# Attention layer of a two-layer trunk: from a hand-woven TensorE order to a list scheduler that orders every queue, and the output projection's depth cut 6 + 2 in place of 7 + 1

## The chip, the cores and the metric

One Trainium2 chip, of which the kernel uses one core. The time is device microseconds of one execution, from the median of several runs. Five engines work side by side, each through a queue of its own: TensorE (PE: matrix products and transposes, with its weight loads PEld), VectorE (DVE), ScalarE (ACT), GpSimd (POOL) and SyncE (SP), which here only starts DMA transfers. What orders them against each other are semaphores.

## The reference

Layer A is gated DeltaNet with a gated ConvFFN, layer B chunked attention with a second ConvFFN. The change lies in the attention of layer B. There `h` is 1024 positions of 1024 channels, 16 heads are 64 wide, and every 64-position chunk sees itself and the eight chunks before it:

```python
kv = rmsnorm(h, kv_norm) @ w_kv
def chunk_attention(xn, w_q, rel_bias, w_out, k_pad, v_pad):
    q = (xn @ w_q).reshape(bsz, nc, CHUNK, B_HEADS, B_HEAD_DIM).transpose(1, 0, 2, 3, 4)
    ...
    def one_chunk(args):
        n, q_n = args
        k_band = lax.dynamic_slice_in_dim(k_pad, n * CHUNK, BAND, axis=1)
        v_band = lax.dynamic_slice_in_dim(v_pad, n * CHUNK, BAND, axis=1)
        s = jnp.einsum("bqhd,bkhd->bhqk", q_n, k_band) * scale + bias
        s = jnp.where(valid, s, NEG_INF)
        p = jax.nn.softmax(s, axis=-1)
        return jnp.einsum("bhqk,bkhd->bqhd", p, v_band)
    ...
    return o @ w_out
h = h + chunk_attention(rmsnorm(h, b_norm[j]), b_w_q[j], b_rel_bias[j], b_w_out[j], k_pad, v_pad)
h = h + conv_ffn(rmsnorm(h, f_norm[layer]), f_w_up[layer], f_conv[layer], f_conv_b[layer], f_w_down[layer])
```

## The kernel before

**Products in three parts.** Every fp32 operand is split into a high part and a low part (the rest). A product is three matmuls, high by high, high by low, low by high: lines L120, L121 and L122 of `dense`, 128x128 weights against 512 columns. `split_w` makes a weight tile's parts: optionally a fold of the norm's gain into the raw weights (L100 on POOL), the high part by ACT (L103), the low part by POOL (L105).

**Attention.** The heads are taken as eight pairs `p`. `queue_kv(p)` queues three dense tiles for each pair, K, Q and V, each of 48 matmuls (two halves `s` of 512 positions, eight blocks of depth); ACT and DVE cut the sums into high and low parts (`post_k`, `post_q`, `post_v`), and V is transposed by PE (L1995). A pair has eight units (head `a` of two, `tp` of four; a unit is two query tiles of 128 positions). For each query tile `scores` makes the scores on PE (L2042, L2043, into the PSUM tile `sc`, of which there is one), the sum with the bias and the row maximum on DVE (L2046), the exponential on ACT (L2048), a reciprocal on DVE (L2049) and the product with it on POOL (L2050, the tile `sS`). `attend` then transposes the shares on PE (L2070, tile `ptp`, two banks), splits them by ACT (L2080, `pTh`) and DVE (L2081, `pTl`), and multiplies by V (L2099, L2100, tile `poT`, one bank). `finish` adds the two halves of `poT` through ACT (L2104, `tm`) and DVE (L2105, `oT`). The first product of a unit can begin only when the `oT` of the unit before has read the one `poT` bank.

**What sets the order.** On PE the order is the program's: the `Weave` puts dense matmuls between a unit's steps by fixed credits (`more`, 1 to 2.2 dense steps of three matmuls at each hook). A pair's three dense tiles may start only once the pair two before it has stored its output (`("o", p - 2)`). ACT, DVE, POOL and SP are ordered by the framework's list scheduler.

**Output projection.** The outputs of pairs 0 to 6 go to DRAM and come back (`early_o`, 12 + 2 loads into the three buffers of the tag `vt`), when pair 5 is done. ACT and DVE or POOL split them (`split_act`, L338, L339). The first part takes seven blocks of depth of eight (`first_parts`, `part`); `rest(s)` adds the eighth when the last pair's half `s` is there: eight sums of three matmuls, each added to `h` on DVE (L459), squared on ACT (L357) and summed on DVE (L359, L367) for the norm before the ConvFFN. Eight tiny matmuls (L370, `pss`) total these sums. Between `rest(0)` and `rest(1)` stand the second halves of four parts.

**The ConvFFN behind it** has an order of its own, all engines in program order. Its first weights `r` are loaded from the POOL queue (L1437, `j == 0`).

Of the kernel before, what the change touches and what calls it, by code (L numbers as in the profile page):

```python
# [16 lines left out]
P = 128  # L17
# [11 lines left out]
def trunk_kernel(  # L29
# [170 lines left out]
    class Flow(Weave):  # L200
# [4 lines left out]
        def __init__(self):  # L205
            super().__init__()
            self.T, self.free, self.aux = 0.0, dict(D=0.0, A=0.0, G=0.0), deque([[0.0], [0.0]])
            self.time, self.items, self.last, self.stalls = {}, [], 0, []
            self.auto, self.tick, self.slack, self.cur, self.nxt, self.units = True, 0, 0.5, None, deque(), 0
            self.brief, self.split_at = False, 8  # L210
# [61 lines left out]
        def _dense(self):  # L272
            if self.cur is None:
# [8 lines left out]
                self.cur, self.split_at, self.units = e[0], e[4], 0  # L282
            try:
                next(self.cur)
            except StopIteration:
                self.cur = None
# [1066 lines left out]
    def ffn(layer, h, hp, xs, tail, d_r, last):  # L1353
# [80 lines left out]
        def load(j, q, t_=None):  # L1434
            t_ = t_ or room(j, q)
            k0, m = 4 * (q % 10 - 1), j if q < 20 else FP + j
            (nc.gpsimd if j == 0 else nc.sync).dma_start(out=t_, in_=w_up[k0 * P : (k0 + 4) * P, m * P : (m + 1) * P].rearrange("(k p) m -> p k m", p=P))  # L1437
# [513 lines left out]
    with ExitStack() as ph:  # L1951
        odd = ctx_o.enter_context(tc.tile_pool(name="bp1", bufs=1, **SB))
        bp = ph.enter_context(tc.tile_pool(name="bp", bufs=1, **SB))
        early_bp = ExitStack()
# [11 lines left out]

        def queue_kv(p):
# [4 lines left out]
            def post_k(s, ps):  # L1972
# [3 lines left out]
                for a, (r, r2) in enumerate(own):  # L1976
                    nc.scalar.copy(kA[a][r, c], ps[r])
                    nc.vector.tensor_tensor(kA[a][r2, c], ps[r], kA[a][r, c].bitcast(F32), op=ALU.subtract)

            def post_q(s, ps):  # L1980
# [4 lines left out]
                for a, (r, r2) in enumerate(own):  # L1985
                    nc.scalar.activation(qA[a][r, c], ps[r], AF.Copy, scale=0.125)
                    nc.vector.scalar_tensor_tensor(qL[a][r, c], ps[r], 0.125, qA[a][r, c].bitcast(F32), op0=ALU.mult, op1=ALU.subtract)
                    nc.vector.tensor_copy(qA[a][r2, c], qA[a][r, c].bitcast(F32))
                if s == 1:
                    wv.mark(("kq", p))  # L1990

            def turn(s, vt):
                pv = pB.tile([P, 4, P], F32, name="pvt", tag="pt", bufs=2)
                for t in range(4):
                    nc.tensor.transpose(pv[:, t], vt[:, t * P : (t + 1) * P], ident)  # L1995
                for a in range(2):
                    vs = kv["v"][a][:, 4 * s : 4 * s + 4, :]
                    src = pv[:, :, 64 * a : 64 * a + 64]
                    nc.scalar.copy(vs[:, :, 0:64], src)
                    nc.vector.tensor_tensor(vs[:, :, 64:128], src, vs[:, :, 0:64].bitcast(F32), op=ALU.subtract)  # L2000
                if s == 1:
                    wv.mark(p)
                yield

            def post_v(s, ps):
# [4 lines left out]
                t0 = wv.now  # L2010
                wv.short.append((lambda: True, lambda: t0 + 3, turn(s, vt)))
# [6 lines left out]
            for src, c0, g, post in ((w_kv, p * P, g_kv, post_k), (b_w_q, p * P, g_b, post_q), (w_kv, 1024 + p * P, g_kv, post_v))[2 if p == 0 else 0 :]:  # L2018
                load = lambda src=src, c0=c0, g=g: load_w(src, c0, fold=g, on_act=p < 1)
                wv.dense.append((lambda: p < 2 or ("o", p - 2) in wv.at, lambda: 0, dense_gen(load, post)))  # L2020
# [10 lines left out]
        def scores(a, t, kA, qA, qL, bt):  # L2031
# [7 lines left out]
            qs = slice(t * P, (t + 1) * P)  # L2039
            for i in range(n):  # L2040
                c = slice(k0 + i * w, k0 + (i + 1) * w)
                mm(ps[:, i, 0:w], qA[a][:, qs], kA[a][:, c], start=True, stop=False)  # L2042
                mm(ps[:, i, 0:w], qL[a][:, qs], kA[a][:, c], start=False, stop=True)  # L2043
            S = bp.tile([P, n, w], F32, name="sS", tag="sS", bufs=6)
# [3 lines left out]
            nc.scalar.activation(S, S, AF.Exp, bias=st[:, 1:2], accum_out=st[:, 2:3])  # L2048
            nc.vector.reciprocal(st[:, 3:4], st[:, 2:3])  # L2049
            nc.gpsimd.tensor_scalar(S, S, st[:, 3:4], 1.0, op0=ALU.mult, op1=ALU.mult)  # L2050
            return S.rearrange("p n w -> p (n w)"), t - nk + 1

        def attend(a, tp, kv, sc, oT, more, tail):

            kt0, kt1 = sc[0][1], 2 * tp + 1
            blocks = [((kt, 0), (kt, 1)) for kt in range(sc[1][1], 2 * tp + 1)]
            if sc[1][1] > kt0:
                blocks.append(((kt0, 0), (kt1, 1)))
            else:
                blocks.append((None, (kt1, 1)))  # L2060
            V = kv["v"]
            po = [None]

            def turn(bl):
                pt = pB.tile([P, 2, 256], F32, name="ptp", tag="pt", bufs=2)
                for j, b in enumerate(bl):
                    for e in b:
                        if e is not None:
                            S, s0 = sc[e[1]]
                            nc.tensor.transpose(pt[:, j, e[1] * P : (e[1] + 1) * P], S[:, (e[0] - s0) * P : (e[0] - s0 + 1) * P], ident)  # L2070
                pTh = bp.tile([P, 2, 256], F32R, name="pTh", tag="pTh", bufs=3)
                pTl = bp.tile([P, 2, 256], F32R, name="pTl", tag="pTl", bufs=3)
                if bl[-1][0] is None:
                    v = [(0, slice(0, 256)), (1, slice(P, 256))] if len(bl) == 2 else [(0, slice(P, 256))]
                    v = [(pt[:, j, c], pTh[:, j, c], pTl[:, j, c]) for j, c in v]
                else:
                    n = len(bl)
                    v = [(pt[:, 0:n], pTh[:, 0:n], pTl[:, 0:n])]
                for s_, h_, l_ in v:
                    nc.scalar.copy(h_, s_)  # L2080
# [239 lines left out]
```

## Time and profile before

| what | us |
|---|---|
| median of 3 runs (2609.0 to 2610.76) | 2609.09 |
| span of the profiled execution | 2612.5 |
| attention, 1371 to 1790 us of the span | 419 |
| change to the output projection, 1790 to 1830 us | 40 |
| projection's end and step to the ConvFFN, 1890 to 1930 us | 40 |
| start of the ConvFFN, 1930 to 2050 us | 120 |

The span is that of one execution under the profiler, from the first to the last instruction; it is 3.4 us above the median of the runs without it. In the views a row names the source line, the engine, the operation, and `out<-in` by the program's tile names. PE's matmuls are pipelined: in a list in order of time, the difference of two starts is what a matmul costs, while the duration beside it includes the pipeline.

### The profile page before, as it was taken

The page shows a single profiled execution, that of the slowest core. Times are in us where ns is not written, and L with a number is a line of the kernel's source. Part 1 is how long each engine was busy: PE and PEld are TensorE (multiplying, and loading weights), DVE is VectorE, ACT ScalarE, POOL GpSimd, SP SyncE. Part 2 cuts the span into 40 slices and gives each one's busy share as a digit, 9 for nine tenths or more (in the row PEclk, how much of TensorE's full clock was granted, in tenths as well). Part 3 has the DMA queues.
Part 4 walks back from the last instruction along what each step waited for, and adds up shares of the span by engine and source line. Part 5 has one row for each costly group of instructions (what it writes and reads, how often), then busy time and mean ns, then how long its engine had stood idle before and what let it go on. Part 6 is the DMA issues. An engine that isn't in the chain of part 4 may idle for free.

```text
span 2612.5 us, 39401 instructions
## 1 busy us (share of the span) xinstructions
PE 2520.3 (96%) x13933; PEld 2075.8 (79%) x13933; DVE 1857.8 (71%) x3102; ACT 1414.5 (54%) x2714; POOL 1486.5 (57%) x1472
## 2 busy tenths in 40 slices
PE   7999999999999999999999999999989999999998
PEld 5878888888777888887778888887867788888877
DVE  5755775454688888888775666666478788888875
ACT  5444555474455565555455555555345655555643
POOL 3655554346347777777645444443343777777771
PEclk9999999999999999999999999999999999999999
DMA  4534445455237777767831111114232567677785
GB/s 128 140 96 120 119 121 164 135 183 160 83 89 153 145 156 153 146 143 158 197 112 51 44 59 43 48 42 145 70 122 68 142 137 150 145 155 156 157 193 174
DMA packets 317590, 326.72 MB, mean 125 GB/s; under 512 B 32976, under 2 KB 240592, under 8 KB 317392
## 3 DMA queue, kind: packets, MB, share of 16 engines
q1 hardware_dynamic: 285936, 219.07, 28.2%
q0 software_dynamic: 26560, 96.48, 20.8%
q10 hardware_dynamic: 4896, 8.65, 0.9%
q8 instruction: 110, 1.80, 0.3%
q14 instruction: 88, 0.72, 0.1%
HBM read 180.94 MB, written 143.20 MB: 124 GB/s over the span
## 4 chain that ended last, share of the span: by engine, by line
PE 52%; DVE 5%; POOL 5%; issue 3%; DMA 2%; ACT 2%; SPq 0%; DVEq 0%; POOLq 0%; ACTq 0%
PE pu L1393 8%; PE pu L1392 8%; PE pu L1391 8%; PE pd L1393 4%; PE pd L1392 4%; PE pd L1391 4%; PE acc L120 3%; PE acc L121 3%; PE acc L122 3%; POOL ul L1358 2%; PE ptp L2070 2%; DMA r<-in_f_w_up_dram 1%; PE poT L2100 1%; PE poT L2099 1%; PE sc L2042 1%
## 5 line engine op out<-in xcount | busy, mean ns | idle before, releaser
L1358 POOL TENSOR_TENSOR ul<-r,uh 128x512 fp32r<-128x512 f32 x282 | 445.1, 1598 | 297.3 <-ACT uh L1379 282.4
L120 PE MATMUL acc<-xh,whi 128*128 128x512 f32 x896 | 375.6, 420 | 0.3 <-ACT xh L1097 0.2
L105 POOL TENSOR_TENSOR wlo<-wraw,whi 128x256 fp32r<-128x256 f32 (+1 forms) x293 | 236.8, 837 | 214.1 <-ACT whi L103 182.8
L122 PE MATMUL acc<-xh,wlo 128*128 128x512 f32 x896 | 353.4, 394 | 3.7 <-POOL wlo L105 3.7
L121 PE MATMUL acc<-xl,whi 128*128 128x512 f32 x896 | 354.1, 395 | 1.9 <-POOL xl L379 1.0
L1379 ACT CAST uh<-r 128x512 fp32r<-128x512 f32 x296 | 181.8, 622 | 222.1 <-DVE r L1358 154.0
L1393 PE MATMUL pu<-xh,ul 128*128 128x512 f32 x552 | 216.5, 392 | 6.2 <-POOL ul L1358 6.1
L1391 PE MATMUL pu<-xh,uh 128*128 128x512 f32 x552 | 216.3, 392 | 3.0 <-ACT uh L1379 1.5
L1392 PE MATMUL pu<-xl,uh 128*128 128x512 f32 x552 | 215.9, 391 | 1.0 <-POOL xl L379 1.0
L122 PEld LDWEIGHTS acc<-xh,wlo 128*128 128x128 f32 x896 | 169.1, 189 | 42.0 <-POOL wlo L105 4.5
L1712 ACT COPY stage<-pd 128x1024 f32<-128x1024 f32 x180 | 175.0, 1013 | 49.4 <-PE pd L1393 49.4
L121 PEld LDWEIGHTS acc<-xl,whi 128*128 128x128 f32 x896 | 170.4, 190 | 27.1 <-DVE xl L1098 3.1
L120 PEld LDWEIGHTS acc<-xh,whi 128*128 128x128 f32 x896 | 170.1, 190 | 23.3 <-ACT xh L1097 1.2
L1486 DVE SCALAR_TENSOR_TENSOR val<-vpre,colt,val 128x1023 f32<-128x1023 f32 (+2 forms) x92 | 153.2, 1665 | 38.6 <-ACT val L1483 38.4
L1358 POOL TENSOR_TENSOR dl<-a,dh 128x512 fp32r<-128x512 f32 x90 | 155.0, 1722 | 38.5 <-ACT dh L1379 38.5
L1486 DVE SCALAR_TENSOR_TENSOR gate<-gpre,colt,gate 128x1023 f32<-128x1023 f32 (+2 forms) x92 | 175.4, 1907 | 0.8
L2050 POOL TENSOR_SCALAR sS<-sS,st 128x640 f32<-128x640 f32 (+4 forms) x128 | 87.8, 689 | 143.1 <-DVE st L2049 122.9
L1358 DVE TENSOR_TENSOR r<-r,r 128x512 f32<-128x512 f32 x168 | 131.8, 784 | 31.1 <-POOL ul L1358 29.7
L2048 ACT ACTIVATE sS<-sS,st 128x640 f32<-128x640 f32 (+4 forms) x128 | 89.2, 696 | 82.0 <-DVE st L2047 80.2
L1393 PEld LDWEIGHTS pu<-xh,ul 128*128 128x128 f32 x552 | 104.0, 188 | 31.7 <-POOL ul L1358 10.4
L1391 PEld LDWEIGHTS pu<-xh,uh 128*128 128x128 f32 x552 | 103.9, 188 | 25.7 <-ACT uh L1379 2.4
L1392 PEld LDWEIGHTS pu<-xl,uh 128*128 128x128 f32 x552 | 104.0, 188 | 23.6 <-POOL xl L379 2.1
(389 smaller groups left out, 7110.0 us busy)
## 6 DMA issues: line engine op xcount, KB each, us to landing
r<-in_f_w_up_dram SPq DMA_DIRECT2D x168, 256.0 KB, 4.2
d_r<-stage POOLq DMA_DIRECT2D x78, 512.0 KB, 7.8
d_c<-stage POOLq DMA_DIRECT2D x70, 512.0 KB, 8.2
a<-in_f_w_down_dram SPq DMA_DIRECT2D x72, 256.0 KB, 2.7
wraw<-in_a_w_in_dram SPq DMA_DIRECT2D x32, 512.0 KB, 4.6
d_e<-stage POOLq DMA_DIRECT2D x32, 512.0 KB, 8.6
wraw<-in_a_w_out_dram SPq DMA_DIRECT2D x16, 512.0 KB, 4.2
d_r<-h ACTq DMA_DIRECT2D x32, 256.0 KB, 4.0
```

The lines of the kernel that those rows point to most:

```text
L105: nc.gpsimd.tensor_tensor(lo[:, c], raw[:, c], hi[:, c].bitcast(F32), op=ALU.subtract)
L120: mm(ps, hi[:, kw, wcol : wcol + P], rh[k][s], start=st, stop=False)
L121: mm(ps, hi[:, kw, wcol : wcol + P], rl[k][s], start=False, stop=False)
L122: mm(ps, lo[:, kw, wcol : wcol + P], rh[k][s], start=False, stop=sp)
L1358: tt = lambda eng, o, a, b, op: eng.tensor_tensor(o, a, b, op=op)
L1379: copy(hi, src)
L1391: mm(ps, w[0][:, cw], x[0], start=first, stop=False, skip_group_check=True)
L1392: mm(ps, w[0][:, cw], x[1], start=False, stop=False, skip_group_check=True)
L1393: mm(ps, w[1][:, cw], x[0], start=False, stop=last, skip_group_check=True)
L1486: nc.vector.scalar_tensor_tensor(t_[:, a:c1], p_[:, a - step : c1 - step], w[:, 2 - step : 3 - step], t_[:, a:c1], op0=ALU.mult, op1=ALU.add)
L1712: nc.scalar.copy(t_, ps)
L2048: nc.scalar.activation(S, S, AF.Exp, bias=st[:, 1:2], accum_out=st[:, 2:3])
```

## The change

The attention and the output projection are now written as generators for `Flow`, the list scheduler that the kernel uses for its first layer. `Flow` keeps a clock `T` of PE work and a time at which DVE, ACT and POOL come free (`on(e, cost)`), and takes, at each point, the highest-ranked item whose inputs it holds to be there, else one dense step. `score_run`, `turn_run` and `apply_run` are three such runs over all 64 units: up to six score tiles and three turned pieces may be open. Low parts are issued when the high part is due (`later`). The order in which items are taken is the program's order on all five queues (`manual_schedule()` without a list of engines).

Beside that:

- K and Q of a pair wait for the scores of the pair two before it (`("scored", p - 2)`), only V for its output. Each weight tile is loaded one tile ahead and split halfway through the tile before it.
- The first V tile's fold moves from ACT to POOL; the low parts of the projection's weights are cut in four pieces.
- The outputs of pairs 0 to 5 are fetched as each is stored, into six buffers of their own (`yo`); pair 6 is split straight from its tile, like pair 7.
- The projection's first part has six blocks of depth (`NO = 6`), `rest(s)` two: eight sums of six matmuls, with weights in two pieces.
- `h` comes back in eight loads of 512 KB in place of sixteen of 256 KB.
- In the second layer the ConvFFN's first four weight loads are started from SP in place of POOL.

The core of the diff:

```diff
-            (nc.gpsimd if j == 0 else nc.sync).dma_start(out=t_, in_=w_up[...])
+            (nc.gpsimd if j + layer == 0 else nc.sync).dma_start(out=t_, in_=w_up[...])
...
+        def kv_tile(src, c0, g, post):
+            raw = wp.tile(shape, F32, name="wraw", tag="wraw", bufs=2)
+            nc.sync.dma_start(out=raw, in_=src[:, c0 : c0 + P].rearrange("(k p) m -> p k m", p=P))
+            yield
+            wt = split_w(raw, shape, fold=g)
+            wv.on("G", 2.75, wv.on("A", 1.0, wv.on("G", 2.6)))
+            yield
+            for s in range(2):
+                ps = pacc.tile([P, HALF], F32, name="acc", tag="acc", bufs=3)
+                for i in range(KT):
+                    dense(ps, wt, 0, xh, xl, FULL[i : i + 1], s, first=i == 0, last=i == KT - 1)
+                    if i < KT - 1:
+                        yield
+                post(s, ps)
+                yield
...
+            def share():
+                nc.vector.reciprocal(st[:, 3:4], st[:, 2:3])
+                t_ = wv.on("D", 0.13)
+                nc.gpsimd.tensor_scalar(S, S, st[:, 3:4], 1.0, op0=ALU.mult, op1=ALU.mult)
+                wv.mark(u, wv.on("G", 0.2 + 1.04e-3 * W, t_))
...
+                if b0 == 0:
+                    yield from wait(*[("v", p, s) for s in range(1 + tp // 2)])
+                    while po_free[0] > wv.T:
+                        yield min(po_free[0], wv.T + 0.5)
+                    po = pacc.tile([P, HALF], F32, name="poT", tag="po", bufs=1)
...
         def early_o(k, s):
-            yt = spare()
+            yt = bp.tile([P, HALF], F32, name="yo", tag="yo", bufs=6)
             nc.sync.dma_start(out=yt, in_=d_o[k][:, hs(s)])
-            split_act(acts, yt, s, k)
+            yield wv.T + 3.0
+            yield from wait("acts")
+            nc.scalar.copy(acts[0][k][s], yt)
...
+        NO = 6
...
+            for m in range(KT):
+                c = m * P // w_
+                ps = pacc.tile([P, HALF], F32, name="acco", tag="acc", bufs=3)
+                for k in range(NO, KT):
+                    dense(ps, wts[c], m * P - c * w_, *acts, [(k - NO, k)], s, first=k == NO, last=k == KT - 1)
...
-        with tc.manual_schedule(engines={mybir.EngineType.PE}):
+        with tc.manual_schedule():
```

The whole computation stays the same, with the same number of matmuls. Three places show how rows move.

**PE, from the last unit of pair 1 to the first of pair 2** (`poT` is the product with V, 128x128 its last pieces in a unit, 128x256 the first of the next; `ptp` and `pvt` are transposes, `sc` scores, `acc` dense work). Before:

```order
L2099 MATMUL poT<-pTh,V 128x128
L2100 MATMUL poT<-pTl,V 128x128
L2070 MATMUL ptp<-ident,sS 128x128 x4
L2042 MATMUL sc<-kA,qA 128x512
L2043 MATMUL sc<-kA,qL_13395 128x512
L2099 MATMUL poT<-pTh,V 128x256
```

The same place in the change:

```order
L2215 MATMUL poT<-pTh,V 128x128
L2216 MATMUL poT<-pTl,V 128x128
L2170 MATMUL ptp<-ident,sS 128x128 x4
L2033 MATMUL pvt<-ident,vt 128x128 x4
L120 MATMUL acc<-xh_0_13085,whi 128x512
L121 MATMUL acc<-xl_0_13086,whi 128x512
L122 MATMUL acc<-xh_0_13085,wlo 128x512
L120 MATMUL acc<-xh_0_13087,whi 128x512
L121 MATMUL acc<-xl_0_13088,whi 128x512
L122 MATMUL acc<-xh_0_13087,wlo 128x512
L2215 MATMUL poT<-pTh,V 128x256
```

Six dense matmuls and four transposes of V now stand between two uses of the one `poT` bank, in place of two score products. Before, some 30 rows around this place hold no dense work; now dense work stands in them throughout.

**DVE, the end of `rest(0)`** (L459 or L2360 adds a projected sum to `h`, L359 or L361 sums the squares for the norm, L367 or L369 is the last such sum, for which `pss` on PE waits). Before:

```order
L459 TENSOR_TENSOR h_5_18465<-acco,h_5_18465 128x512
L359 TENSOR_TENSOR nacc<-nacc,spare 128x512
L459 TENSOR_TENSOR h_6_18466<-acco,h_6_18466 128x512
L359 TENSOR_TENSOR nacc<-nacc,spare 128x512
L459 TENSOR_TENSOR h_7_18467<-acco,h_7_18467 128x512
L359 TENSOR_TENSOR nacc<-nacc,spare 128x512 x4
L367 TENSOR_TENSOR nacc<-nacc,spare 128x512
```

In the change:

```order
L361 TENSOR_TENSOR nacc<-nacc,spare 128x512
L2360 TENSOR_TENSOR h_5_18599<-acco,h_5_18599 128x512
L2360 TENSOR_TENSOR h_6_18600<-acco,h_6_18600 128x512
L361 TENSOR_TENSOR nacc<-nacc,spare 128x512
L2360 TENSOR_TENSOR h_7_18601<-acco,h_7_18601 128x512
L361 TENSOR_TENSOR nacc<-nacc,spare 128x512 x3
L2298 TENSOR_TENSOR h_4_18598<-acco,h_4_18598 128x512
L369 TENSOR_TENSOR nacc<-nacc,spare 128x512
```

The sums stand in nearly the same order, but the last one now comes behind the end of the first part that follows (L2298); on PE each `h` add stands for six matmuls in place of three.

**POOL, one weight tile in the middle of the attention** (L100 folds, L105 makes low parts, L2050 or L2125 multiplies the shares by the reciprocal). Before:

```order
L105 TENSOR_TENSOR wlo<-wraw,whi 128x256 x4
L2050 TENSOR_SCALAR sS<-sS,st 128x640
L100 TENSOR_TENSOR wraw<-wraw,colt 128x256 x4
L2050 TENSOR_SCALAR sS<-sS,st 128x640 x2
L2027 MEMSET bt 64x64
L2028 MEMSET bt 64x64
L2050 TENSOR_SCALAR sS<-sS,st 128x128
L2050 TENSOR_SCALAR sS<-sS,st 128x256
L105 TENSOR_TENSOR wlo<-wraw,whi 128x256 x4
```

In the change:

```order
L2125 TENSOR_SCALAR sS<-sS,st 128x640
L100 TENSOR_TENSOR wraw<-wraw,colt 128x256 x4
L105 TENSOR_TENSOR wlo<-wraw,whi 128x256 x4
L2125 TENSOR_SCALAR sS<-sS,st 128x640
L2078 MEMSET bt 64x64
L2079 MEMSET bt 64x64
L2125 TENSOR_SCALAR sS<-sS,st 128x640 x2
```

The low parts now follow their fold directly, with no product of shares in between; POOL reaches them before ACT has made the high part that stands between the two.

More of the change, by code (lines that the diff above doesn't have):

```diff
@@ L1953, in trunk_kernel @@
         bp = ph.enter_context(tc.tile_pool(name="bp", bufs=1, **SB))
+        for _ in range(3):
+            bp.tile([P, HALF], F32, name="vt", tag="vt", bufs=3)
         early_bp = ExitStack()
@@ L2123, in units @@
[L2123 to L2138 removed]
+            sc_free[0] = t0 = wv.on("D", 0.35 + 1.04e-3 * W)
@@ L2226, in trunk_kernel @@
+        env["cut"] = 1
     ctx_o.close()
```

419 lines of the change are left out of this document (271 added, 148 removed).

## The prediction

> **What bounds the kernel now.** I began with the page's table of engines, then cut the span into stages, asked in each what PE waits for, and went to the rows in order of time at the longest waits. The table gives PE the span:
>
> ```profile
> PE 2520.3 (96%) x13933; PEld 2075.8 (79%) x13933; DVE 1857.8 (71%) x3102; ACT 1414.5 (54%) x2714; POOL 1486.5 (57%) x1472
> ```
>
> The number of matmuls does not change, so all that can be won or lost is time in which PE waits or runs slowly. The stages (us, PE, PEld, DVE, ACT, POOL busy, PE's granted clock, DMA):
>
> ```profile
> 1371.00:1790.00 419.00, 407.41 (x2329) 345.71 (x2329) 259.30 (x775) 236.72 (x554) 189.57 (x307) 1.00 0.16 48
> 1790.00:1830.00 40.00, 34.40 (x174) 28.73 (x174) 22.20 (x68) 23.38 (x58) 15.37 (x17) 0.87 0.66 215
> 1830.00:1890.00 60.00, 60.00 (x318) 50.89 (x317) 23.75 (x54) 20.95 (x39) 22.95 (x16) 1.00 0.20 56
> 1890.00:1910.00 20.00, 14.54 (x58) 12.14 (x57) 12.13 (x17) 8.01 (x12) 3.56 (x2) 0.74 0.46 152
> 1930.00:2050.00 120.00, 108.85 (x465) 83.94 (x463) 103.35 (x125) 66.32 (x101) 48.61 (x33) 1.00 0.30 97
> ```
>
> In the attention PE is idle for 419.00 - 407.41 = 11.6 us, at the change to the projection for 5.6, at the projection's end for 5.5. The first 120 us of the ConvFFN lose 11.2, with DVE busy for 103 of 120: that is the ConvFFN's own order, which is not touched. Who is waited for, first in the attention, then from 1790 to 1935 us:
>
> ```profile
> PE poT L2099 <- DVE oT L2105: 5.7, 7, 1.0
> PE ptp L2070 <- POOL sS L2050: 2.2, 4, 0.7
> PE ptp L2070 <- DVE st L2047: 1.4, 5, 0.3
> ...
> PE pss L370 <- DVE nacc L367: 5.5, 1, 5.5
> PE acco L120 <- ACT xh L338: 3.8, 1, 3.8
> PE pu L1393 <- POOL ul L1358: 2.3, 1, 2.3
> PE acc L122 <- POOL wlo L105: 0.5, 1, 0.5
> PE acco L122 <- POOL wlo L105: 0.9, 1, 0.9
> ```
>
> Half of the attention's waits are one wait, seven times 0.8 us: the product with V for the one `poT` bank. The rest are a few big ones at the seams. Ten-microsecond slices add what a slower clock takes:
>
> ```profile
> 1430.00:1440.00 10.00, 8.29 (x54) 6.99 (x53) 6.18 (x22) 6.38 (x17) 4.80 (x10) 1.00 0.11 34
> 1800.00:1810.00 10.00, 6.21 (x21) 5.01 (x22) 4.92 (x16) 5.64 (x14) 4.38 (x6) 0.67 0.74 220
> 1810.00:1820.00 10.00, 10.00 (x49) 8.47 (x48) 5.31 (x15) 4.52 (x11) 4.33 (x4) 0.85 0.65 210
> 1900.00:1910.00 10.00, 8.59 (x31) 7.54 (x32) 2.55 (x4) 0.84 (x2) 0.72 (x1) 0.57 0.16 47
> ```
>
> After the waits of 3.8 and 5.5 us the granted clock falls, by 0.33 + 0.15 of 10 us = 4.8 us at the first seam, by 0.43 of the 8.6 busy us = 3.7 at the second. The slice that holds shorter waits (1.7 us in all) stays at 1.00. [...] The sum below takes the measured slices.
>
> **The change part by part.** A dense matmul costs the difference of two starts, 0.23 us; a product with V 0.12, four transposes 0.36:
>
> ```profile
> 1496.18 0.39 PE L120 MATMUL acc<-xh,whi 128*128 128x512 f32 x1
> 1496.40 0.40 PE L121 MATMUL acc<-xl,whi 128*128 128x512 f32 x1
> ...
> 1497.10 0.28 PE L2099 MATMUL poT<-pTh,V 128*128 128x256 f32 x1
> 1497.22 0.28 PE L2100 MATMUL poT<-pTl,V 128*128 128x256 f32 x1
> 1497.34 0.60 PE L2070 MATMUL ptp<-ident,sS 128*128 128x128 f32 x4
> 1497.70 0.43 PE L2042 MATMUL sc<-kA,qA 128*128 128x384 f32 x1
> ```
>
> *1. The `poT` bank and the turned pieces.* I counted, in the built order, the PE work between two uses of a buffer at these prices. Between the end of one unit's products with V and the next unit's first, seven places held 0.7 to 0.9 us before, and seven waits of 0.8 us on average followed: the turn through ACT and DVE takes about 1.7. In the change the shortest such distance is 1.9 us, the next 2.3. From the transposes to the products that use them, 25 of 144 places held under 3 us; now none does (shortest 3.2), against a turn of about the same 1.7. So the 5.7 us go. Of the transposes' 2.2 + 1.4 + 0.6 us I let half go, since they hang on POOL and DVE, whose queues are reordered; the 1.6 us of small waits that are left I keep. Term: -7.8. At best all 11.6 go; at worst none (rivals).
>
> *2. The change to the projection.* Before, twelve outputs come back from DRAM through three buffers, after pair 5:
>
> ```profile
> 1809.20 0.62 ACT L338 CAST xh<-spare 128x512 fp32r<-128x512 f32 x1 [1.34 <-DMA spare<-d_o]
> ...
> 1798.65 1.27 POOL L339 TENSOR_TENSOR xl<-spare,xh 128x512 fp32r<-128x512 f32 x1 [0.98 <-ACT xh L338]
> ```
>
> Six now lie there when the last V tile ends, and each later one has a buffer when an earlier one is split. What stays is the chain from that last tile: copy, split and low part of 0.6 to 0.7 us each, some 2.4 us with the handovers and exponentials of 0.8 between them, against 3.7 us of counted PE work, then POOL's low parts of odd blocks (1.27 us each, two per block) against 4.1 us of PE work per two blocks. I leave 2.4 of the 5.6 + 4.8 = 10.4 us. Term: -8.0; bounds -10.4 and 0 (if the split stays as late).
>
> *3. The end of the projection.* Before, eight sums of three matmuls pass in 8 x 0.68 = 5.4 us, while DVE needs sixteen steps:
>
> ```profile
> 1889.19 4.09 DVE L459 TENSOR_TENSOR h<-acco,h 128x512 f32<-128x512 f32 x6
> 1895.61 3.07 DVE L359 TENSOR_TENSOR nacc<-nacc,spare 128x512 f32<-128x512 f32 x4
> ```
>
> 16 x 0.68 = 10.9 us, so PE, which stops at `pss`, waits. With six matmuls per sum PE takes 8 x 1.36 = 10.9 us, the same as DVE, and the 5.5 us of extra work are taken from the first parts: nothing is added. The last sum now stands behind the end of the next part, 18 matmuls later; `pss` comes three matmuls (0.7 us) after that, and DVE then needs 0.2 + 0.69 + 0.68: 0.9 us stay. Term: 5.5 + 3.7 - 0.9 = -8.3. Bounds: -9.2 and 0.
>
> *4. The ConvFFN's first weights.* Before, POOL starts the loads only after its last split, and reaches the first cast late:
>
> ```profile
> 1925.09 3.12 POOL L1437 DMA_DIRECT2D r<-in_f_w_up_dram  x4
> 1930.98 0.61 POOL L1379 CAST uh<-r 128x512 fp32r<-128x512 f32 x1 [1.73 <-DMA r<-in_f_w_up_dram]
> ```
>
> On SP they stand directly behind the last two weight loads, which go out when the second-last part is split, over 10.9 us (`rest(1)`) ahead. The 2.3 us go, and of the 0.9 on a late low part half: -2.7. Bounds: -3.2 and 0.
>
> *5. The start of the attention.* Before, 36 dense matmuls of V (8.2 us) stand between the last K and Q work and the first score; now six (1.4 us). The K and Q parts end on DVE here, and the first score is read much later:
>
> ```profile
> 1371.30 0.68 DVE L1987 SCALAR_TENSOR_TENSOR qL<-acc,qA 64x512 fp32r<-64x512 f32 x1 [0.27 <-ACT qA L1986]
> 1373.37 0.80 DVE L1988 CAST qA<-qA 64x512 fp32r<-64x512 f32 x1
> 1379.05 0.29 DVE L2046 CUSTOM_DVE_ANT_0 sS<-sc,bt 128x128 f32<-128x128 f32 x1 [4.89 <-issue]
> ```
>
> DVE ends them at 1374.2; the first score is then read at 1374.5, and the second, which needs the one `sc` tile and could be made at 1373.2, waits some 1.4 us. Term: +1.4; bounds 0 and +3. The displaced dense work is used later, in place of the stretches without any. The first V tile's fold on POOL is issued between the two earlier tiles' splits and hidden behind 11 us of K and Q matmuls.
>
> *6. Costs I take as nothing.* Four pieces in place of one for the projection's low parts cost some tenths each on a POOL that is busy 57%; without the cover of a split half a tile ahead they would delay a tile by that much. The loads of `h` carry the same bytes, and each stands at least a tile (4 us) ahead of its use. If that lead were gone, DVE would hold at the load, and the `acc` banks behind it.
>
> Sum: -7.8 - 8.0 - 8.3 - 2.7 + 1.4 = -25.4. Against the execution's own 2612.5: 2587.1. That execution is 3.4 us above the runs' median, 2609.09, so 2583.7: I say 2584.
>
> **The rivals.** *POOL's queue closes, slower.* In program order a weight tile holds POOL from the start of its fold to the end of the low parts, and every share product behind them waits:
>
> ```profile
> L105 POOL TENSOR_TENSOR wlo<-wraw,whi 128x256 fp32r<-128x256 f32 x84 | 59.7, 743 | 30.1 <-ACT whi L103 16.2 <-PE ptp L2070 13.8
> L100 POOL TENSOR_TENSOR wraw<-wraw,colt 128x256 f32<-128x256 f32 x80 | 47.1, 618 | 69.0 <-DMA wraw<-in_w_kv_dram 45.1 <-DMA wraw<-in_b_w_q_dram 23.9
> L103 ACT CAST whi<-wraw 128x1024 fp32r<-128x1024 f32 x20 | 21.0, 1050 | 9.9 <-PE acc L121 9.1 <-ACT sS L2048 0.6
> L2050 POOL TENSOR_SCALAR sS<-sS,st 128x640 f32<-128x640 f32 x56 | 45.5, 817 | 65.7 <-DVE st L2049 63.0 <-DVE st L2047 1.6 <-PE sc L2043 1.1
> L2046 DVE CUSTOM_DVE_ANT_0 sS<-sc,bt 128x640 f32<-128x640 f32 x56 | 45.9, 820 | 7.0 <-PE sc L2043 6.7
> L2048 ACT ACTIVATE sS<-sS,st 128x640 f32<-128x640 f32 x56 | 46.5, 830 | 36.3 <-DVE st L2047 34.6 <-POOL wraw L100 1.7
> ...
> wraw<-in_w_kv_dram SPq DMA_DIRECT2D x13, 512.0 KB, 4.0
> ```
>
> Fold 4 x 0.62, high part 1.05, low parts 4 x 0.74: 6.5 us, and the softmax chain 0.82 + 0.83 + 0.82 with its small steps some 3.0. The counted distance from a unit's last score to its first transpose is 10.7 us in the median, so PE waits from the point where a fold starts more than 1.2 us late. Before, folds wait 69 us for their loads, 3.45 per tile. If they do so with shares queued behind them, 22 tiles lose 3.45 - 1.2 each: +49.5 - 25.4 = +24, about 2633. Against it: the load is issued six dense steps (4.1 us) and the attention work among them before the fold, and a load lands in 4.0 us, as the list of transfers has it; the fold's waits before are those of a POOL that has little else to do. [...]
>
> *Waits are moved, not removed.* If the attention keeps its 11.6 us under other names, term 1 goes: 2592. If term 2 goes as well, because splitting twelve outputs next to the softmax keeps ACT and POOL late: 2600. For it speaks that the first seam's ACT holds exponentials among the casts.
>
> *The ConvFFN takes it back, no change.* DVE is at 103 of 120 us behind the seam. If it, and not PE's arrival, sets the ConvFFN's first stage, terms 3 and 4 are given back there; with terms 1 and 2 at half, 7.9 - 1.4 = 6.5 are left, and a little less makes it no change, 2603 to 2609. Against it: DVE is busy for only 12.1 of the 20 us before, so it can move ahead with PE.
>
> **How the numbers follow.** Forecast 62% (2584, own range 2574 to 2592); waits moved 20% (2592 to 2603); given back 6%; POOL's queue 12% (from no change up to 2633). The lowest is 2609.1 - 11.6 - 10.4 - 9.2 - 3.2 = 2574.7. Range: 2574 to 2605. Of the measurement some 0.2%, 5 us, can't be told from no change: faster 0.82, same 0.07, slower 0.11.
>
> **What would show it.** Right: no wait of PE for `oT`, PE idle under 5 us in the attention, no granted clock under 0.9 between the attention's start and the ConvFFN, `pss` waiting 1 us or less, and the first `pu` row not waiting for POOL. Wrong: PE's transposes waiting for POOL's shares tens of times, POOL's fold waiting for loads, or idle time in the ConvFFN's first 120 us growing by what the projection wins.

## The result, and the profile after

| | before | changed |
|---|---|---|
| median, us | 2609.93 | 2593.62 |
| lowest to highest, us | 2609.0 to 2617.19 | 2593.14 to 2597.97 |
| span of the profiled execution, us | 2612.5 | 2591.4 |

The ratio is 0.9938 (95% interval 0.9923 to 0.9953): the change gains 16.3 us, where 25.4 were forecast. The two profiled executions differ by more, 21.1 us. A span leaves out some 1.7 us that a run's time counts (2591.4 against 2593.14 for the same run of the changed kernel), so the changed kernel's trace lies close to its median and the one of before 4 to 5 us above its own. Of the 21.1 us, 2.4 stand ahead of the attention, in a part that the change does not touch. What follows from the traces is weighed against the 21.1.

The table of engines again gives PE the span, now with 78 us of the span not busy in place of 92:

```profile
PE 2513.5 (97%) x13933; PEld 2078.2 (80%) x13933; DVE 1856.7 (72%) x3102; ACT 1410.0 (54%) x2708; POOL 1494.1 (58%) x1517
```

The stages of the changed kernel (us, PE, PEld, DVE, ACT, POOL busy, PE's granted clock, DMA), shifted to where the same work now stands: attention, change to the projection, projection's end, step to the ConvFFN, its first 120 us.

```profile
1380.00:1780.00 400.00, 398.55 (x2338) 347.92 (x2337) 256.75 (x772) 236.81 (x558) 189.72 (x312) 1.00 0.17 50
1780.00:1815.00 35.00, 29.58 (x136) 23.74 (x134) 21.16 (x61) 20.06 (x49) 18.36 (x21) 0.85 0.35 113
...
1840.00:1900.00 60.00, 54.98 (x253) 43.55 (x252) 26.13 (x40) 21.99 (x33) 31.70 (x42) 0.99 0.41 136
1900.00:1920.00 20.00, 19.62 (x90) 16.02 (x89) 14.23 (x19) 7.98 (x14) 12.35 (x10) 0.95 0.73 227
1920.00:2040.00 120.00, 111.84 (x467) 86.63 (x466) 103.49 (x125) 68.00 (x102) 49.84 (x32) 0.99 0.28 91
```

The attention is almost closed: 1.45 us idle, where 11.6 were. The change to the projection is not: 35.00 - 29.58 = 5.4 us idle, and a clock of 0.85 takes 0.15 x 29.58 = 4.4 more, 9.8 in place of the prediction's 10.4 (10.1, if before is counted from its stage's row in the same way). At the end 5.0 us are idle, and 10-us slices show 0.93 and 0.90 between 1890 and 1910 us, 1.6 us more: 6.6 in place of 9.2. The ConvFFN's start loses 8.2 us, less than before. Whom PE waits for, in the attention's first 30 us, in the rest of it, then from 1780 to 1900 us (us, times, longest):

```profile
PE sc L2109 <- DVE qL L2020: 2.3, 1, 2.3
...
PE pvt L2033 <- ACT vt L2052: 1.4, 7, 0.2
...
PE acco L120 <- ACT whi L103: 5.3, 4, 2.7
PE acco L121 <- POOL xl L2266: 1.9, 2, 1.6
PE acco L122 <- POOL wlo L105: 1.3, 2, 0.7
PE acco L120 <- DVE h L2298: 1.0, 2, 0.8
PE pss L372 <- DVE nacc L369: 0.9, 1, 0.9
```

No wait for `oT`, none of a transpose for POOL: the attention went as predicted. Behind it the old waits are gone (`acco` for `xh`, 3.8 us) or small (`pss`, 0.9 us in place of 5.5), and a new one stands in their place: the high part of a weight tile, made by ACT. ACT's list in order of time shows why the first comes late:

```profile
1780.08 3.21 ACT L2263 CAST xh<-yo 128x512 fp32r<-128x512 f32 x6
1783.19 0.65 ACT L2037 CAST V<-pvt 128x256 fp32r<-128x256 f32 x2
1783.72 0.74 ACT L2119 ACTIVATE sS<-sS,st 128x512 f32<-128x512 f32 x1
...
1785.72 0.84 ACT L103 CAST whi<-wraw 128x768 fp32r<-128x768 f32 x1
```

The six outputs that lie ready in `yo` are cast in one go, 3.21 us, as soon as their tiles exist; everything else in ACT's queue, exponentials and the projection's second weight tile among it, stands behind them in program order. PE has 3 x 2 matmuls of the first tile and then waits 2.7 us. That became the theory: program order by the list scheduler pays on PE and inside the attention; on ACT it costs what the two seams should have won.

### The profile page after: what moved, and what is told of

The parts are those of the page before. It is cut to its first block, busy times and chain, and to the rows that moved or that the text cites. A ratio compares the mean times of both kernels' runs of the same rounds, so it can differ in the third digit from the quotient of the medians.

```text
span 2591.4 us, 39359 instructions
## 1 busy us (share of the span) xinstructions
PE 2513.5 (97%) x13933; PEld 2078.2 (80%) x13933; DVE 1856.7 (72%) x3102; ACT 1410.0 (54%) x2708; POOL 1494.1 (58%) x1517
## 5 line engine op out<-in xcount | busy, mean ns | idle before, releaser
L105 POOL TENSOR_TENSOR wlo<-wraw,whi 128x256 fp32r<-128x256 f32 (+3 forms) x338 | 248.8, 767 | 206.0 <-ACT whi L103 178.1
L2125 POOL TENSOR_SCALAR sS<-sS,st 128x640 f32<-128x640 f32 (+4 forms) x128 | 86.4, 680 | 206.5 <-DVE st L2123 197.6
L2114 DVE CUSTOM_DVE_ANT_0 sS<-sc,bt 128x640 f32<-128x640 f32 (+4 forms) x128 | 84.1, 657 | 132.5 <-PE sc L2110 87.1
L2183 ACT CAST pTh<-ptp 128x512 fp32r<-128x512 f32 (+2 forms) x176 | 75.4, 452 | 89.7 <-PE ptp L2170 86.3
```

Of the source, the lines that this page charges most:

```text
L105: nc.gpsimd.tensor_tensor(lo[:, c], raw[:, c], hi[:, c].bitcast(F32), op=ALU.subtract)
```

## The experiments

All times are medians; each ratio is to runs of the kernel before on the same chip (2610.8 to 2611.9 us there). Differences to the changed kernel are between medians from different chips; a ratio's interval is some 3 to 4 us to either side.

### The depth alone: 6 + 2 on the kernel before, 7 + 1 on the changed one

On the kernel before (pair 6 still comes back from DRAM):

```diff
-                b_w_out, h, 7, 6, d_r1, add_h, ...
+                b_w_out, h, 6, 6, d_r1, add_h, ...
...
-            for k in range(soon, n):
+            for k in range(soon, 7):
```

> The kernel before with one part of the change alone: depth 6 + 2 in place of 7 + 1 in the projection (outputs of pair 6 still come back from DRAM; order on PE in the attention is the same). Theory from the changed kernel's trace (weight waits take the place of the pss wait): -1 to -5 us, 2605 to 2609. Rival, the forecast's term 3 at its full size: -8.3 us, about 2601.6. In the trace: pss waits 1 us or less under both; under the theory PE's waits for whi and wlo grow by 3 us or more between the parts.

Measured: 2602.3 us, ratio 0.9968 (0.9956 to 0.9980), 8.5 us faster. Its wait at `pss`:

```profile
PE pss L370 <- DVE nacc L367: 1.0, 1, 1.0
```

No wait for `whi` took its place. The forecast's term of 8.3 us, with 0.9 left, agrees with the median (the interval runs from 5.2 to 11.5 us); the theory read from the changed kernel's trace (1 to 5 us) fell. So 6 + 2 is worth 8.5 us where the framework orders ACT, DVE and POOL, and the changed kernel's weight waits are not the price of 6 + 2.

On the changed kernel:

```diff
-        NO = 6
+        NO = 7
...
-            for n, (k, s) in enumerate([(k, s) for k in range(NO) for s in range(2)]):
+            for n, (k, s) in enumerate([(k, s) for k in range(6) for s in range(2)]):
...
-                if m == 0:
+                if m == 0 and KT - NO > 1:
```

> The changed kernel with the projection's depth cut 7 + 1 again in place of 6 + 2 (eight sums of three matmuls in rest(s), one weight piece); all else as changed. Changed kernel 2593.6 us. Theory from the changed kernel's trace: the 5.5 us wait at pss and the 3.7 us of clock went, but short waits for weights of about the same size (whi and wlo, 3.9 us, and 1.6 us of clock) came between the parts; with 7 + 1 the parts are longer (21 matmuls, 4.8 us per load), so those weight waits shrink while pss stalls again: net +1 to +5 us, 2595 to 2599. Rival (the forecast's term 3 at its full size): +8.3 us, about 2602. A third, that pss no longer stalls because DVE's order is now the program's: no change or faster.

Measured: 2612.1 us, ratio 1.0004 (0.9994 to 1.0014). Undoing the depth costs 18 us, more than twice any expectation, and the whole gain. From 1840 us on PE waits, in that kernel:

```profile
PE acco L120 <- ACT whi L103: 8.2, 3, 2.9
PE pu L1393 <- POOL uh L1381: 3.9, 1, 3.9
PE pss L372 <- DVE nacc L369: 3.7, 1, 3.7
```

`pss` is the term that was undone. The 8.2 us are a loop through three queues, read from one list for each, of DVE, ACT and PE:

```profile
1894.82 0.69 DVE L2298 TENSOR_TENSOR h<-acco,h 128x512 f32<-128x512 f32 x1 [6.19 <-PE acco L122]
1895.42 0.74 DVE L392 SCALAR_TENSOR_TENSOR h<-h,colt,psb 128x512 f32<-128x512 f32 x1
```
```profile
1896.20 0.62 ACT L393 CAST xh<-h 128x512 fp32r<-128x512 f32 x1 [6.92 <-DVE h L392]
1896.72 0.93 ACT L103 CAST whi<-wraw 128x896 fp32r<-128x896 f32 x1
```
```profile
1897.71 0.50 PE L120 MATMUL acco<-xh,whi 128*128 128x512 f32 x1 [2.93 <-ACT whi L103]
```

DVE holds at the sum of a part that PE has not finished; the norm's step behind it, which could run (PE made its `psb` by 1885.8 us), waits; ACT holds at that step's cast; the next part's weights stand behind the cast; PE, done with its part, waits for them. It comes round three times. In the changed kernel the same neighbours stand in ACT's queue, with smaller waits:

```profile
1885.36 0.62 ACT L393 CAST xh<-h 128x512 fp32r<-128x512 f32 x1 [3.60 <-DVE h L392]
1885.88 0.82 ACT L103 CAST whi<-wraw 128x768 fp32r<-128x768 f32 x1
```

### Which queue's order, and where

First all queues but PE's back to the framework, for attention and projection (PE's order stays the same, row for row):

```diff
-        with tc.manual_schedule():
+        with tc.manual_schedule(engines={mybir.EngineType.PE}):
```

> The changed kernel with only PE in the program's order; DVE, ACT, POOL and SP ordered by the framework's list scheduler again, as before. Theory: the attention's gain comes from PE's new order (distances between a buffer's uses), so most of the 16 us stays: 2590 to 2597, and the burst of six casts on ACT at the projection's start may be broken up by the framework. Rival: the gain comes from the other queues' order (short waits of PE that the counted distances don't show, some 8 us): 2600 to 2609. The forecast's rival of a closing POOL queue, turned round: if program order on POOL costs, this one is faster than 2590.

Measured: 2590.0 us, ratio 0.9917 (0.9904 to 0.9929). With PE alone in program order, and all other parts of the change as they are, the whole gain is there, by the medians 3.6 us more (the two intervals just overlap). No wait for `oT` is left in its attention, so PE's order is enough to remove those. Its stages, attention, change to the projection, projection's end:

```profile
1380.00:1780.00 400.00, 393.17 (x2278) 340.01 (x2276) 252.80 (x756) 232.07 (x545) 181.82 (x299) 1.00 0.16 51
1780.00:1815.00 35.00, 32.60 (x188) 27.64 (x189) 23.74 (x77) 22.28 (x59) 18.09 (x21) 1.00 0.47 169
1840.00:1900.00 60.00, 59.86 (x291) 50.08 (x290) 32.00 (x48) 24.93 (x38) 31.34 (x39) 1.00 0.35 110
```

Against the changed kernel the attention loses 5.4 us of idle time (6.8 in place of 1.45), both seams win, and the clock stays at 1.00. Since PE's order is the same in both, one can also go from one matmul to the same one: from the norm's tiny matmuls ahead of the attention to a matmul at 1756 us this kernel takes 9.7 us longer, and up to the tiny matmuls at the norm's end it is 5.9 us shorter. So program order was kept up to the last V tile's sums and given up behind them:

```diff
+            wv.run(lambda: "acts" in wv.time)
+        with tc.manual_schedule(engines={mybir.EngineType.PE}):
             wv.run(lambda: not (wv.dense or wv.items or wv.late or wv.cur or wv.nxt))
```

> The changed kernel with all queues in the program's order only until the last V tile's sums are copied; from there on only PE is, and the framework orders DVE, ACT, POOL and SP. Changed kernel 2593.6 us, and with only PE in program order throughout 2590. Theory: program order pays in the attention (PE's short waits there, against ideal matmul costs: 11.6 us with all queues in order, 18 with PE alone) and costs at the projection's two seams (19 us against 6): so 2582 to 2587, with no PE wait for whi there. Rival: the attention's rest of 6 to 7 us is chance and follows from other things: 2588 to 2592, as with PE alone.

Measured: 2581.3 us, ratio 0.9882 (0.9869 to 0.9895), 12 us under the changed kernel, and no PE wait for `whi`. That is just past the theory's range (2582 to 2587) and well past the rival's. Its change to the projection, and from there to 1900 us:

```profile
1780.00:1815.00 35.00, 32.08 (x166) 27.60 (x164) 21.72 (x69) 18.35 (x47) 15.91 (x23) 0.90 0.41 155
1815.00:1900.00 85.00, 84.67 (x427) 71.28 (x426) 46.98 (x77) 36.64 (x61) 43.86 (x55) 1.00 0.33 102
```

Then ACT alone, by naming PE, DVE, POOL and SP in that second list (DVE's order moves by two instructions):

> The changed kernel with ACT alone given back to the framework's order from the last V tile on; PE, POOL and SP keep the program's order throughout, and DVE but for two instructions. It tells which queue's order costs the changed kernel (2593.6 us) its two seams, of which freeing ACT, DVE, POOL and SP together won 12 us (2581.3). Theory: it is ACT's, where the second weight tile's split stands behind six casts of returned outputs and the later splits behind casts of the norm that wait for DVE: most of it comes back, 2582 to 2587, and PE's waits for whi fall from 5.3 us to 1 us or less. Rival: it is DVE's, where the sums that wait for PE stand ahead of the norm's steps, or POOL's: 2588 to 2593.

Measured: 2583.5 us, ratio 0.9892 (0.9875 to 0.9908). By the medians ten of the twelve us are ACT's queue. From the tiny matmuls ahead of the attention to those at the norm's end the traces give 569.1 us for the changed kernel, 562.0 here and 558.4 with all queues freed: 7 of 11. PE waits no longer for `whi`; what is left there is POOL's:

```profile
PE acco L121 <- POOL xl L2266: 3.0, 2, 2.7
...
PE acco L122 <- POOL wlo L105: 1.6, 3, 1.2
```
```profile
1780.00:1815.00 35.00, 29.74 (x150) 23.71 (x150) 22.64 (x60) 17.68 (x43) 21.06 (x23) 0.95 0.41 131
1815.00:1900.00 85.00, 83.64 (x411) 69.97 (x410) 42.72 (x72) 33.64 (x56) 42.82 (x54) 0.98 0.39 126
```

The first seam is as idle as in the changed kernel (5.3 us): freeing ACT wins there by the clock and by matmuls done sooner, 2.7 us up to the matmul that stands at 1813.5 us in the changed kernel. The other 4.4 come behind it.

Last, 7 + 1 on the kernel of 2581.3 us, to split the 18 us:

> The depth cut 7 + 1 again, on top of the kernel whose queues other than PE are the framework's from the projection on (2581.3 us with 6 + 2). It tells apart why 7 + 1 cost 18 us with all queues in program order. Theory: those 18 us are the forecast's term of 8.3 us (measured at 8.5 us by the depth cut alone on the kernel before) and some 10 us of weight splits that the program's order on ACT and POOL places late, which the framework here does not: 2587 to 2592. Rival: PE's own order with 7 + 1 is bad by 18 us whoever orders the others: 2597 to 2602.

Measured: 2591.8 us, ratio 0.9926 (0.9912 to 0.9941): 10.5 us, with `pss` waiting 3.3 us, the first `pu` 3.1 us for POOL's `uh`, and no wait for `whi`. Of the 18 us some 10 are depth and some 8 the closed loop, each by a difference of medians that is good to a few us.

### The two seams by hand, in program order

The second weight tile's split ahead of the six casts (called where the last V sum has been copied, in place of at the first part's start):

```diff
                     act_tiles((0, 1), acts)
                     wv.mark("acts")
+                    ahead[0]()
...
+            ahead.append(lambda: wts.append(part_split(raws[1])))
             yield 20
-            wts.append(part_split(raws[1]))
```

> The changed kernel with one ACT and POOL job moved: the projection's second weight tile is split as the last V tile's second sum has been copied, ahead of the six casts of returned outputs, in place of behind them. The attention's order on PE is the same. Theory (the 2.7 us wait for whi and about 3 us of clock behind it come from that place in ACT's queue): -3 to -6 us against the changed kernel's 2593.6, so 2588 to 2591. Rival (ACT is simply full there; the casts are late by 0.8 us instead and PE waits for xh or xl): 2592 to 2595.

Measured: 2591.5 us, ratio 0.9928 (0.9916 to 0.9941), which can't be told from the changed kernel's 0.9938. PE's waits from 1780 to 1815 us:

```profile
PE acco L121 <- POOL xl L2267: 3.7, 1, 3.7
PE ptp L2171 <- POOL sS L2126: 2.0, 1, 2.0
PE acco L120 <- DVE h L2299: 1.6, 1, 1.6
```

The 2.7 us for `whi` are gone and 3.7 for a low part on POOL have come, as the rival had it, only on another engine: moving one tile's split in a fixed order moved the wait.

The first score later, so that it finds its `qL`:

```diff
                     for s in range(2):
                         post(s, ps[s])
+                wv.mark(("kq", 0), 12.0)
```

> The changed kernel with the first score held back until four more dense steps (12 matmuls, 2.7 us) of the first V tile are done: 18 matmuls in place of 6 stand before it. Changed kernel 2593.6 us. Theory: the 2.3 us wait of the first score for qL goes, -2 us, 2590 to 2593. Rival: the planner's whole order behind it moves too (one place with 0.45 us between uses of poT, one stretch of 6.3 us without dense work), which takes it back or more: 2593 to 2598.

Measured: 2584.2 us, ratio 0.9896 (0.9884 to 0.9909), 9.5 us under the changed kernel, where 2 were expected. The 2.3 us wait is gone; the rest came at the change to the projection, which fell elsewhere in the planner's order and lost its long wait and its slow clock:

```profile
1780.00:1815.00 35.00, 34.24 (x194) 29.32 (x193) 24.32 (x67) 18.90 (x46) 16.71 (x22) 1.00 0.32 106
```

The casts still go six in a row there (3.23 us); the second tile's split follows a little sooner, and PE waits 0.9 us for it. So what the seam costs in program order depends on where the planner happens to arrive.

### The gate of K and Q alone, and the loads from POOL

On the kernel before, K and Q wait for the scores of the pair two before it, V for its output:

```diff
-                wv.dense.append((lambda: p < 2 or ("o", p - 2) in wv.at, lambda: 0, dense_gen(load, post)))
+                wv.dense.append((lambda n=n: p < 2 or (("scored", "o")[n == 2], p - 2) in wv.at, lambda: 0, dense_gen(load, post)))
...
+                if (a, tp, i) == (1, 3, 1):
+                    wv.mark(("scored", p))
```

> The kernel before with one part of the change alone: K and Q of a pair wait for the scores of the pair two before it, only V for its output. PE's order then has three places instead of seven with under 1 us of work between two uses of the poT bank, and six more at 1.6 us. Kernel before 2609.9 us. Theory that the counted distances set the waits, with a turn of about 1.7 us: 3 waits of about 0.8 us instead of 7, -3 us, 2605 to 2609; the attention's other short waits stay. Rival: the gate is the whole of the attention's gain (dense work at the change of pairs): -12 to -20 us, 2590 to 2598. Rival: no change, since the stretches without dense work are only moved.

Measured: 2624.0 us, ratio 1.0049 (1.0036 to 1.0062), 13 us slower; every expectation fell. PE's waits from 1380 to 1820 us:

```profile
PE sc L2044 <- DVE st L2048: 14.5, 17, 3.5
PE pvt L1995 <- ACT vt L2009: 6.9, 5, 1.4
PE poT L2101 <- DVE oT L2107: 3.8, 4, 1.7
```

`poT` has fewer waits, as counted, but the dense work let in early is missing later. The stretches without any last some 11 us at four changes of pair, where they were 7.7 in the kernel before, and 29 us (1790.8 to 1820.0) at the last, where they were 9.2; in them scores wait for the one `sc` tile. So the gate alone costs; that it pays together with the planner is argued, since no run has the planner without it.

On the changed kernel, the second ConvFFN's first loads from POOL again:

```diff
-            (nc.gpsimd if j + layer == 0 else nc.sync).dma_start(out=t_, in_=w_up[...])
+            (nc.gpsimd if j == 0 else nc.sync).dma_start(out=t_, in_=w_up[...])
```

> The changed kernel with the second ConvFFN's first four weight loads started from POOL again, as before the change. Changed kernel 2593.6 us. Forecast's term 4: +2.7 us, about 2596, with the first pu waiting some 2 us or more for POOL's ul or uh. Rival: the ConvFFN's first 120 us are set by DVE, so it is taken back there: 0 to +1 us.

Measured: 2601.8 us, ratio 0.9965 (0.9952 to 0.9978), 8.2 us over the changed kernel by the medians (6.8 by the spans), two to three times the term. POOL's list and PE's, then PE's slice:

```profile
1907.12 3.13 POOL L1439 DMA_DIRECT2D r<-in_f_w_up_dram  x4
1912.87 1.12 POOL L1381 CAST uh<-r 128x512 fp32r<-128x512 f32 x1 [2.62 <-DMA r<-in_f_w_up_dram]
```
```profile
1914.04 0.80 PE L1393 MATMUL pu<-xh,uh 128*128 128x512 f32 x1 [3.48 <-POOL uh L1381]
1916.37 0.80 PE L1395 MATMUL pu<-xh,ul 128*128 128x512 f32 x1 [1.11 <-POOL ul L1360]
```
```profile
1910.00:1920.00 10.00, 5.41 (x14) 3.55 (x13) 4.21 (x7) 3.06 (x5) 6.89 (x7) 0.66 0.90 285
```

4.6 us of waits and 0.34 x 5.41 = 1.8 of clock. PE reaches the first `pu` 3.4 us after POOL starts the loads (1907.1 to 1910.5), in the kernel before 5.3 us after (1925.1 to 1930.4), so late loads cost more here than the 2.3 us they cost there.

### The edits that gained, together

Program order up to the last V sums, PE alone behind, and the later first score:

> The two edits that gained, together: all queues in program order only until the last V tile's sums are copied, then PE alone; and 18 dense matmuls ahead of the first score in place of 6. Alone they stand at 2581.3 and 2584.2 us, against 2593.6 of the changed kernel. Theory: the start's 2.3 to 2.9 us add to the first edit, and what the second won at the projection's first seam (6 us by its trace) overlaps with it in part: 2574 to 2579. Rival, the second edit's gain was mostly a lucky place of the seam, which the first edit has taken already: 2580 to 2583.

Measured: 2576.3 us, ratio 0.9860 (0.9846 to 0.9873): 35.5 us under the kernel before and 17 under the changed one. Attention, change, end:

```profile
1380.00:1780.00 400.00, 395.16 (x2316) 345.60 (x2315) 263.96 (x774) 240.37 (x569) 201.89 (x323) 1.00 0.18 55
1780.00:1815.00 35.00, 34.06 (x193) 29.45 (x192) 20.55 (x63) 16.11 (x40) 11.02 (x19) 1.00 0.43 155
1840.00:1900.00 60.00, 59.69 (x277) 49.03 (x276) 37.96 (x54) 27.50 (x41) 38.45 (x42) 1.00 0.48 149
```

With the early split of the second tile besides:

> The kernel with both edits and the projection's second weight tile split as the last V tile's second sum is copied. Theory: the framework already moves that split, so it changes little: within 2 us of the kernel with both edits. Rival: it still stands late on ACT, PE waits behind it and the clock falls: 3 to 6 us faster than with both edits.

Measured: 2575.7 us, ratio 0.9857 (0.9841 to 0.9874), no difference, as expected: where the framework orders ACT, that place makes no difference that these runs can tell.

## Why the prediction was right, and where it was not

The direction and the range held; the number was 9.6 us too low, and 2593.62 lies 1.6 us past the forecast's own range, in that of "waits are moved". The terms beneath it were off by more than their sum, and in both directions: the attention gave more than was said and the two seams less, so that the total came so close is in part luck.

| step | forecast, us | in the changed kernel | by experiment |
|---|---|---|---|
| 1 attention | -7.8 | -10.1 idle, some -15 in all | PE's order alone: no wait for `oT` |
| 2 change to the projection | -8.0 | -0.3 to -0.6 | both seams, against the changed kernel: -10 with ACT freed, -12 with all |
| 3 projection's end | -8.3 | -2.6 | -8.5 alone, before |
| 4 ConvFFN's first loads | -2.7 | first `pu` not waiting | undone: +8.2 |
| 5 start of the attention | +1.4 | +2.3 | first score later: -9.5, most of it at the first seam |

**Step 1 was too small.** The counted distances held: no wait for `oT`, none for shares. But the term took the idle time of the page as all there was. A dense matmul takes 0.39 us in the list and starts 0.23 after the last, so a wait of up to 0.16 us is covered by the modelled end and shows no idle time. From the norm's tiny matmuls before the attention to those at its end, the changed execution is 20.2 us shorter (589.3 to 569.1); the visible parts there (10.1 in the attention, 0.6, 2.6, 3.2 at the first `pu`, 1.1 before the first score, less the 2.3 at it) make 15.3, so 5 show nowhere. That they are short waits is argued: a count of differences of starts against medians gives 11 to 21 us for the attention, as one takes the median of each pair of neighbouring kinds of matmul or of each kind, and the order itself changes which kinds are neighbours. PE's order removes the waits for `oT`, as the run with PE alone shows; but that run also takes some 9 us more in the attention, so a good part of the gain there hangs on the order of the other queues, to which the step gave 2.1 us (half of 4.2). No run took one distance back alone.

**Step 2 failed.** It left 2.4 us and 9.8 stayed. It gave "copy, split and low part of 0.6 to 0.7 us each" to the one last V tile, on an ACT with a few exponentials between. The six outputs that the step itself says lie ready are cast in one piece of 3.21 us in the same queue, and the second weight tile waits behind them.

The step's 4.8 us of clock hold a wrong reading too. Part of the half clock before stands ahead of the wait of 3.8 us (1804.1 to 1807.9), behind three short waits of 0.25 to 0.66 us:

```profile
1799.40:1802.80 3.40, 3.40 (x16) 3.19 (x15) 2.00 (x7) 1.92 (x6) 1.07 (x3) 0.50 0.76 222
```

The sum counts no clock for the waits it leaves, and no run shows that it may: in the changed kernel three waits of 0.53 to 0.72 us were followed by a clock of 0.51, and the one of 0.90 us at `pss` by 1.00.

**Step 3** was right about DVE, PE and `pss` (0.9 us, as written); it left out ACT's queue, in which the next part's weights stand behind the norm's casts. ACT's queue is the larger part of what both lost: with its order alone given back 10 us return by the medians, 7 by the traces; with all queues 12 and 11. At the first seam it is not all: with ACT freed PE waits 2.7 us there for POOL's low part, and with the second tile's split moved ahead 3.7 us for the same. In program order the step's 8.0 us came back only with the later first score, and there unplanned; which order would bring them on purpose stays open.

**Step 4** was right in kind, and its undoing shows that its price depends on how early PE comes. **Step 5** had the sign and 0.9 us too little, but not the place: the wait is the first score's for `qL` itself, not the second's for the `sc` tile. **Step 6**'s loads of `h`: one stood behind weight loads on SP and held DVE for 5.5 us at 1865 us; PE then waited 0.2.

**The rivals.** The closing queue, given 12% and placed on POOL, is what happened, mainly on ACT, at the seams only, and at some 7 to 10 us in place of 49.5; POOL's folds kept their lead in the attention. "Waits are moved" is the same thing seen from PE; the measured time lies in its range, but not by its way, which let the attention keep its 11.6 us. The ConvFFN took little back: from the last of those tiny matmuls to the last matmul 668.2 us, 666.4 before.

Of what the prediction said it would show: attention idle 1.45 us (under 5), `pss` 0.9 (1 or less), no wait of the first `pu`, all as written; the granted clock, which was to stay at 0.9 or more, fell to 0.79 (10-us slice from 1780 us).

## What to carry to other kernels

In this kernel a planner's order on every queue paid in the attention, a steady loop, and cost at the seams, where several items become ready at once and a late one blocks ready ones behind it. There it was better to let the framework order the other queues and to keep PE's order. Before pricing a wait that goes, list what else becomes ready at that moment on the engine that must deliver next, in queue order. And test a part on its own in both kernels: the same depth cut was worth 8.5 and 10.5 us, which the noise does not tell apart, where the framework ordered the other queues, and 18 us in program order.

## What the runs showed of the hardware

In the changed kernel the granted clock was half behind waits of 2.73 us (ended at 1786.6) and of 1.64 and 0.28 (ended at 1798.4 and 1799.7):

```profile
1786.00:1789.00 3.00, 2.39 (x7) 2.10 (x8) 0.00 (x0) 2.31 (x5) 2.36 (x5) 0.50 0.75 250
1789.00:1792.00 3.00, 3.00 (x10) 2.35 (x9) 2.43 (x8) 1.42 (x3) 1.82 (x2) 0.50 0.89 267
...
1799.50:1802.50 3.00, 2.81 (x9) 2.22 (x9) 0.00 (x0) 0.00 (x0) 3.00 (x4) 0.51 0.01 3
```

And with 7 + 1, behind the wait of 2.93 us that ended at 1897.7:

```profile
1899.00:1902.00 3.00, 3.00 (x9) 2.32 (x8) 0.44 (x1) 0.00 (x0) 3.00 (x4) 0.50 0.14 18
```

A dense matmul then starts every 0.43 us in place of 0.23. In these runs the length of a wait alone did not decide it. With the loads from POOL, PE waited 2.74 us at the same place (1785.3 to 1788.0), and the clock stayed at 1.00:

```profile
1788.00:1791.00 3.00, 2.65 (x12) 1.90 (x13) 1.19 (x4) 2.29 (x6) 2.97 (x5) 1.00 0.75 236
```

Within the changed kernel the wait of 0.90 us at `pss` (ended at 1880.4) left the clock at 1.00, and three waits of 0.53, 0.62 and 0.72 us close together (ended at 1895.9, 1897.2 and 1898.9) were followed by half:

```profile
1880.00:1890.00 10.00, 8.75 (x45) 6.97 (x46) 4.49 (x7) 3.06 (x6) 3.21 (x5) 1.00 0.14 39
...
1898.50:1902.00 3.50, 3.11 (x7) 2.48 (x8) 0.69 (x1) 1.21 (x2) 3.17 (x4) 0.51 0.20 74
```

So a wait cost its length alone in some places and slower work on top in others; what decides it is not shown here. Around the end of the wait of 2.73 us that was, by the prediction's way of counting, an estimate of 0.50 x 6.09 = 3.0 us:

```profile
1785.90:1792.70 6.80, 6.09 (x17) 5.03 (x18) 3.13 (x9) 4.53 (x9) 4.20 (x6) 0.50 0.83 260
```
